# A streaming-encoder trunk on one core: the order of the transfers in the feed-forward is fixed by hand

## The chip, the core and the metric

The kernel runs on one core of a Trainium2 chip. A core has five engines that work side by side, each through its own queue of instructions: TensorE (PE: matrix products, with its weight loads shown as PEld), VectorE (DVE), ScalarE (ACT), GpSimd (POOL) and SyncE (SP), which here does nothing but issue transfers from the chip's memory into the core's buffer. An engine begins an instruction when the one before it has gone and the semaphores that it waits for have been reached. The metric is the time of one execution on the device, in microseconds (us).

## The reference

```
DEPTH, D_MODEL, D_FF, SEQ = 2, 1024, 2816, 512
for i in range(DEPTH):
    h = rmsnorm(x, mix_norm[i])
    x = x + (pool_mixer(h, ...) if i % 2 == 0 else chunk_attention(h, ...))
    h = rmsnorm(x, ffn_norm[i])
    x = x + conv_ffn(h, ffn_w_gate[i], ffn_w_val[i], ffn_conv_w[i], ffn_conv_b[i], ffn_w_out[i])

def conv_ffn(h, w_gate, w_val, conv_w, conv_b, w_out):
    a = h @ w_gate                                    # (512, 1024) @ (1024, 2816)
    ap = pad(a, two frames in front)
    a = ap[:, 0:S] * conv_w[0] + ap[:, 1:S+1] * conv_w[1] + ap[:, 2:S+2] * conv_w[2] + conv_b
    return (silu(a) * (h @ w_val)) @ w_out            # (512, 2816) @ (2816, 1024)
```

One batch of 512 frames goes through two layers: a pooling mixer, a feed-forward, a chunked attention, a second feed-forward. Everything is in 32-bit floats. The change concerns the two feed-forwards only.

## The kernel before, in words

The activations lie channel by channel: X[0] to X[7] hold 128 channels by 512 frames each. To keep 32-bit accuracy, every operand of a product is split into a high part and a low part (ACT copies the high part, line 409, and DVE subtracts it for the low part, line 410), and a product is the sum of up to three matmuls: high by high, high by low, low by high (lines 123 to 125).

A feed-forward (`ffn`) has 22 tiles of 128 hidden channels. Of each tile f come two outputs, the gate and the value, from two weight blocks `gv[l, f, 0]` and `gv[l, f, 1]` of 512 KB. From the sixth tile on both outputs are computed together by a scheme of seven half-size products (`strassen`). It works in named steps: `load` issues the two transfers into the buffers `gv_r`, `s1` to `s4` build sums of the weight blocks on DVE, `h1` to `h4` copy the high parts on ACT, `l1` to `l4` make the low parts on DVE, `b11`, `b21`, `t1`, `t2`, `t3`, `t4`, `b22` are the products on PE (lines 610 and 612), and `a1`, `v1`, `x1` are ACT's copies of the bank `st_m` (line 619, into `a`, `v` and `w`) between the products that add into that bank: `t1` may start only when `v1` has read it. `a3` (line 763) copies the last half and `a4` (line 768) adds to it on DVE. `c0` to `c6` are the convolution, the silu and the split of the result (lines 421 to 435).

The second product of the feed-forward (`output`) runs in four groups of hidden tiles, `OUT = ((0, 5), (5, 6), (11, 6), (17, 5))`, each with eight blocks of 128 output channels. A block needs a weight transfer of 320 or 384 KB (`wo_r`), its high part on ACT (`ow_h`, line 409) and its low part on DVE (`ow_l`, line 410), then 15 or 18 matmuls (`out`), and an addition to X on DVE (line 817). These blocks are strewn among the products of the later tiles: `tour` yields at the points of a tile, and behind each point the loop takes as many matmuls of the waiting group as `due` says. A block's transfer and its high part are issued in the program when the block before it begins; its low part comes two tiles of matmuls later.

The order of work is set in three ways. What stands in a block `tc.manual_schedule(engines=...)` keeps the order of the program on the engines named. For the rest a planner chooses: it lays out the program against its own model of time and issues on each queue what is ready there. Buffers come from pools with a set number of copies: three for `gv_r` (tag `wr`), one for `wo_r` in the first three groups (tag `or`), two for `ow_h` and two for `ow_l`; a transfer into a buffer waits until the last reader of what was there has finished. For `gv_r` of tile f + 1 that is `s4` of tile f (line 675) and `l4` of tile f - 1 (line 721); for the next `wo_r` it is the low part of the block before (line 410).

PE is in fixed order through the whole feed-forward. The order within a tile is written by hand in `PLACES`, seven places to a tile, where q, o, f and n stand for the tile two before, the one before, this one and the next:

```
PLACES = ("o.x1 q.c5 f.s2 o.x2 f.s3 o.x3 f.b11", "f.a1 f.h2 f.s4 o.l4 q.c6 n.load o.b22", "o.a3 f.h3 f.l2 o.a4 f.b21", "o.c0 f.a2 f.l3 f.a5 o.t4",
          "n.h1 f.h4 o.c1 o.v3 o.c2 o.v4 f.t2", "f.v1 o.c3 n.l1 f.v2 f.t3", "n.s1 o.c4 f.t1")
```

From the first place of tile 8 (`ORDERED`) to the fourth place after the last tile, DVE and ACT also keep this order. SP does not: there the planner chooses.

Of the kernel before, what the change touches and what calls it, by code (L numbers as in the profile page):

```python
# [72 lines left out]
def trunk(ctx: ExitStack, tc: tile.TileContext, xt, xT, cols, band, edge, poolw, gv, wout, wqk, wv, wo, rel, out):  # L73
# [291 lines left out]
    ET = mybir.EngineType  # L365
# [15 lines left out]
    def ffn(l, first, pool, acc, summed=None):  # L381
# [140 lines left out]
        def plain(f):  # L522

            o = []
            for i in range(2):
                with ExitStack() as after:
                    if f < 4:
                        for x in (made, seed) if l == 0 else (known if f == 2 and i == 0 else made,):
                            after.enter_context(tc.issue_after(x.ins))
                    hi, lo = ready[f][i] if f in ready else weights(f, i)  # L530
                o.append(psum("S", f"gv{l}_{f}_{i}", 4))
                for k in range(KD):
                    s = slice(k * P, (k + 1) * P)
                    mm = run(mm3(o[i], hi[:, s], lo[:, s], *(slots[c][4 * (k % 4) + k // 4] for c in range(2)), k == 0, k == KD - 1))
                    if k % 2 and k < KD - 1:
                        yield mm
                if i == 0:
                    yield mm
            run(hidden(f, o[0], lambda c: nc.vector.tensor_mul(c, o[1], c)))
            yield mm  # L540
# [280 lines left out]
        def tour():  # L821

            tiles = {}

            def steps_of(f):
                if f not in tiles:
                    tiles[f] = strassen(f) if f < NF and KIND[f - 1] == "s" else {}
                return tiles[f]

            def place(f, k):  # L830

                for word in PLACES[k].split():
                    x, name = word.split(".")
                    step = steps_of(f + "qofn".index(x) - 2).get(name)
                    if step:
                        step()

            for f in range(KIND.index("s"), NF + 2):
                if f == KIND.index("s"):
                    for g in range(f):  # L840
                        if KIND[g] == "p":
                            yield from plain(g)
                    for j, _ in enumerate(apart(f)):
                        for k, name in ((2, "load"), (4, "h1"), (5, "l1"), (6, "s1")):
                            if j == k:
                                steps_of(f + 1)[name]()
                        yield
                    continue
                for k in range(7):
                    if (f, k) == (ORDERED, 0):  # L850
                        order.enter_context(tc.manual_schedule(engines={ET.DVE, ET.Activation}))
                    place(f, k)
                    if steps_of(f - 1 if k in (1, 3) else f):
                        yield
                    if (f, k) == (NF, 3):
                        order.close()

        with tc.manual_schedule(engines={mybir.EngineType.PE}):
            h, seed, known, made = early()
            queue, left, n = [], 0, 0  # L860
            order = ExitStack()
# [7 lines left out]
            seq += [(NF - 1, False), (NF - 1, True)]  # L869
            ends = [seq.index((b + m - 1, True)) + 1 for b, m in OUT]  # L870
            steps = tour()
            for g, (b, m) in enumerate(OUT):
                points = ends[g] - (ends[g - 1] if g else 0)
# [354 lines left out]
```

## Time and profile before

| | |
|---|---|
| time, median of 3 runs | 991.06 us (989.55 to 991.6) |
| the profiled execution | 991.02 us, of which the span from the first to the last instruction is 989.2 us |
| first feed-forward, ordered stretch | about 127 to 331 us of the span |
| second feed-forward, ordered stretch | about 726 to 931 us of the span |
| PE, DVE, ACT busy | 968.9, 805.4, 573.8 us |
| granted TensorE clock, mean | 0.993 |

A row of the timeline gives the start in us from the span's beginning, the duration in us, the engine (SPq is SP's queue, where the duration is that of the issue alone), the line of the kernel, the operation, what is written and read, the shapes, how many instructions the row joins, and in brackets the idle time of the engine before the row with what ended it. A row of the waits reads: who waited for whom, us in total, how often, the longest. A row of the windows gives a stretch, its length, the busy time of PE, PEld, DVE, ACT and POOL with their counts, the granted clock as a share of full speed, the share of the DMA engines that was busy, and GB/s.

### The profile page before, as it was taken

To read this page: it belongs to the slowest core of one execution; us is meant where nothing else is said; L and a number is where in the kernel's file an instruction comes from. 1 tells how busy PE (TensorE), PEld (TensorE's weight loads), DVE (VectorE), ACT (ScalarE), POOL (GpSimd) and SP (SyncE) were. 2 spreads that over 40 slices of the span, in tenths; PEclk is the share of its full clock that TensorE was granted. 3 is DMA by queue.
4 is the path that set the end of the run, shared out by engine and by line. 5 is a ranking of instruction groups with operands and counts; after the bars stand their busy time and mean duration, and the time that the engine had idled before them with its cause. 6 is when DMAs were issued, how large, how long until landed. Compare 5 with 4: busy or idle time off the path is not lost.

```text
span 989.2 us, 13813 instructions
## 1 busy us (share of the span) xinstructions
PE 968.9 (98%) x5038; PEld 822.3 (83%) x5038; DVE 805.4 (81%) x1452; ACT 573.8 (58%) x990; POOL 103.2 (10%) x90
## 2 busy tenths in 40 slices
PE   8999999899989999999999999999999899989998
PEld 7788988788878888888888787888988788878886
DVE  8999989799879854442777887899979899879953
ACT  7665565565546444345898987656545465446531
POOL 2300000000000013204535441000000000000000
PEclk9999999999999999999999999999999999989999
DMA  8222332332323224232343242332423223222323
GB/s 336 80 86 81 100 112 86 104 115 93 102 75 117 72 83 148 89 123 87 117 125 96 84 116 75 99 107 78 126 70 115 101 83 125 75 101 75 104 84 112
DMA packets 37428, 102.83 MB, mean 104 GB/s; under 512 B 4432, under 2 KB 7904, under 8 KB 37360
## 3 DMA queue, kind: packets, MB, share of 16 engines
q1 hardware_dynamic: 37296, 101.90, 31.5%
q8 instruction: 40, 0.66, 0.3%
q14 instruction: 28, 0.23, 0.1%
q0 software_dynamic: 32, 0.04, 0.0%
q10 hardware_dynamic: 32, 0.00, 0.0%
HBM read 95.60 MB, written 2.14 MB: 99 GB/s over the span
## 4 chain that ended last, share of the span: by engine, by line
PE 91%; DVE 5%; ACT 2%; issue 1%; DMA 0%; DVEq 0%; ACTq 0%
PE st_m L610 9%; PE out L125 8%; PE out L123 8%; PE out L124 8%; PE st_t L610 5%; PE st_m L612 5%; PE gv L124 4%; PE gv L123 4%; PE gv L125 4%; PE qk L124 3%; PE qk L123 3%; PE qk L125 3%; PE st_b L610 3%; PE st_t L612 2%; PE tp L1059 2%; PE oo L1071 2%
## 5 line engine op out<-in xcount | busy, mean ns | idle before, releaser
L409 ACT ACTIVATE ow_h<-wo_r 128x640 fp32r<-128x640 f32 (+1 forms) x64 | 50.5, 788 | 81.3 <-PE out L124 47.2
L125 PE MATMUL out<-one,ow_l 128*128 128x512 f32 x224 | 88.2, 394 | 5.6 <-DVE ow_l L410 5.6
L123 PE MATMUL out<-one,ow_h 128*128 128x512 f32 x224 | 88.1, 393 | 0.0
L124 PE MATMUL out<-one,ow_h 128*128 128x512 f32 x224 | 88.0, 393 | 0.0
L817 DVE TENSOR_TENSOR X<-out,X 128x512 f32<-128x512 f32 (+1 forms) x65 | 44.2, 681 | 49.8 <-PE out L125 49.3
L610 PE MATMUL st_m<-two,g_h 128*128 128x512 f32 x224 | 70.0, 394 | 0.0
L610 PE MATMUL st_m<-h,g_h 128*128 128x512 f32 x224 | 69.1, 389 | 0.0
L410 DVE TENSOR_TENSOR ow_l<-wo_r,ow_h 128x640 fp32r<-128x640 f32 (+1 forms) x64 | 56.6, 885 | 2.6 <-ACT ow_h L409 2.6
L424 DVE SCALAR_TENSOR_TENSOR c<-a,col,c 128x511 f32<-128x511 f32 (+1 forms) x76 | 56.4, 745 | 0.0
L125 PEld LDWEIGHTS out<-one,ow_l 128*128 128x128 f32 x224 | 42.4, 189 | 12.7 <-DVE ow_l L410 6.5
L125 PE MATMUL qk<-wqk_h,two 128*128 128x512 f32 x128 | 51.4, 402 | 0.0
L123 PE MATMUL qk<-wqk_h,two 128*128 128x512 f32 x128 | 50.8, 409 | 0.0
L124 PE MATMUL qk<-wqk_l,two 128*128 128x512 f32 x128 | 50.8, 397 | 0.0
L610 PEld LDWEIGHTS st_m<-h,g_h 128*128 128x128 f32 x224 | 42.1, 188 | 9.6
L612 PEld LDWEIGHTS st_m<-two,g_l 128*128 128x128 f32 x224 | 42.0, 188 | 8.9
L610 PEld LDWEIGHTS st_m<-two,g_h 128*128 128x128 f32 x224 | 41.1, 188 | 9.3 <-ACT w L619 0.8
L619 ACT ACTIVATE w<-st_m 128x512 f32<-128x512 f32 x28 | 16.7, 597 | 54.2 <-PE st_m L612 54.2
L124 PEld LDWEIGHTS out<-one,ow_h 128*128 128x128 f32 x224 | 42.5, 190 | 6.3 <-DVE one L435 0.3
L123 PEld LDWEIGHTS out<-one,ow_h 128*128 128x128 f32 x224 | 42.5, 190 | 6.0
L1047 DVE CUSTOM_DVE_ANT_0 sb<-sc,B 128x128 f32<-128x128 f32 (+1 forms) x64 | 31.1, 486 | 18.8 <-PE sc L1044 18.1
L612 PE MATMUL st_m<-h,g_l 128*128 128x256 f32 x224 | 45.1, 283 | 0.0
L148 POOL TENSOR_TENSOR n_acc<-n_acc,n_sq 128x512 f32<-128x512 f32 x7 | 9.6, 1366 | 336.1 <-ACT n_sq L146 336.1
(378 smaller groups left out, 3027.2 us busy)
## 6 DMA issues: line engine op xcount, KB each, us to landing
gv_r<-gv SPq DMA_DIRECT2D x86, 512.0 KB, 3.8
wo_r<-wout SPq DMA_DIRECT2D x32, 384.0 KB, 3.1
wo_r<-wout SPq DMA_DIRECT2D x32, 320.0 KB, 2.9
wqk_r<-wqk SPq DMA_DIRECT2D x16, 512.0 KB, 3.5
wv_r<-wv SPq DMA_DIRECT2D x8, 512.0 KB, 3.4
wo_r<-wo SPq DMA_DIRECT2D x8, 512.0 KB, 3.4
xt<-xt SPq DMA_DIRECT2D x4, 512.0 KB, 5.7
X<-xT SPq DMA_DIRECT2D x8, 256.0 KB, 7.6
```

The lines of the kernel that those rows point to most:

```text
L123: yield nc.tensor.matmul(o, sh, mh, start=first, stop=False, **how)
L124: yield nc.tensor.matmul(o, sh, ml, start=False, stop=False, **how)
L125: yield nc.tensor.matmul(o, sl, mh, start=False, stop=last, **how)
L409: nc.scalar.activation(hi[:, :n], raw[:, :n], AF.Copy)
L410: return hi, lo, lambda: nc.vector.tensor_sub(lo[:, :n], raw[:, :n], hi[:, :n].bitcast(F32))
L424: nc.vector.scalar_tensor_tensor(c[:, j:], a[:, :S - j], cw[2 - j], c[:, j:], op0=OP.mult, op1=OP.add)
L610: nc.tensor.matmul(o, hi[:, c], B[i, name], start=first and i == 0, stop=False, **how)
L612: nc.tensor.matmul(o[:, 0], lo[:, c], B[i, name][:, 0], start=False, stop=i == 3, **how)
L817: nc.vector.tensor_add(X[d][:, fs], o[:, fs], X[d][:, fs])
L1047: nc.vector.tensor_tensor_reduce(out=s_[:, :n], in0=sc[:, :n], in1=BT[h % 2][:, :n][:, ::-1], scale=1.0, scalar=3e38, op0=OP.add, op1=OP.m ...
L1059: nc.tensor.transpose(tp[:, j * P:(j + 1) * P], s_[:, j * P:(j + 1) * P], ident)
L1071: nc.tensor.matmul(oo[:, j * P:], V[j, h // 4][:, h % 4].rearrange("p a d -> p (a d)"), PT[e][c][:, 4 * j:3 * j + TT].rearrange("p t q -> ...
```

## The change

SP joins DVE and ACT in the block that fixes the order, so the transfers that are issued there, the pairs `gv_r` and the blocks `wo_r`, keep the order in which the program names them. The stretch is the same as before, in both feed-forwards.

```
                 for k in range(7):
                     if (f, k) == (ORDERED, 0):
-                        order.enter_context(tc.manual_schedule(engines={ET.DVE, ET.Activation}))
+                        order.enter_context(tc.manual_schedule(engines={ET.DVE, ET.Activation, ET.SP}))
                     place(f, k)
```

More of the change, by code (lines that the diff above doesn't have):

```diff
@@ L850, in tour @@
                     if (f, k) == (ORDERED, 0):
-                        order.enter_context(tc.manual_schedule(engines={ET.DVE, ET.Activation}))
+                        order.enter_context(tc.manual_schedule(engines={ET.DVE, ET.Activation, ET.SP}))
                     place(f, k)
```

## The prediction

> **What bounds the kernel now.** I read the first part of the page (busy time by engine), then the waits of PE between 127 and 331 us, the stretch that the change covers in the first of the two feed-forward layers.
>
> ```profile
> PE 968.9 (98%) x5038; PEld 822.3 (83%) x5038; DVE 805.4 (81%) x1452; ACT 573.8 (58%) x990; POOL 103.2 (10%) x90
> PE out L125 <- DVE ow_l L410: 5.6, 2, 2.8
> 203.00:266.00 63.00, 63.00 (x328) 53.81 (x327) 58.77 (x95) 34.72 (x50) 0.00 (x0) 1.00 0.31 105
> ```
>
> The first row: PE works 98% of the span. The second row, of the waits: in that stretch PE stands still twice, 2.8 us each, and both times for DVE's low part of the first weight block of an output group; nothing else stops it. The third, of the windows (PE, PEld, DVE, ACT, POOL busy): over four tiles PE is busy all 63 us and DVE 58.77, so DVE has 63.00 - 58.77 = 4.23 us to spare, 1.06 a tile; ACT is idle nearly half the time. No transfer bounds anything here. So the change can gain little, and what it can lose is the head start of the transfers.
>
> **The order on the transfers' row now.** The timeline of SP, the same stretch (a row joins several issues; the number behind x counts them):
>
> ```profile
> 160.99 0.33 SPq L391 DMA_DIRECT2D wo_r<-wout  x1
> 171.06 15.12 SPq L391 DMA_DIRECT2D gv_r<-gv  x4
> 187.28 17.08 SPq L391 DMA_DIRECT2D wo_r<-wout  x3
> 204.60 0.93 SPq L391 DMA_DIRECT2D gv_r<-gv  x2
> 214.30 0.33 SPq L391 DMA_DIRECT2D wo_r<-wout  x1
> 218.24 0.93 SPq L391 DMA_DIRECT2D gv_r<-gv  x2
> 244.18 0.33 SPq L391 DMA_DIRECT2D wo_r<-wout  x1
> 248.97 0.93 SPq L391 DMA_DIRECT2D gv_r<-gv  x2
> 256.34 0.33 SPq L391 DMA_DIRECT2D wo_r<-wout  x1
> 265.81 15.34 SPq L391 DMA_DIRECT2D gv_r<-gv  x4
> ...
> 760.47 0.33 SPq L391 DMA_DIRECT2D wo_r<-wout  x1
> 770.53 15.12 SPq L391 DMA_DIRECT2D gv_r<-gv  x4
> ```
>
> I counted the program's order out of `PLACES`, `seq`, `ends`, `WAIT` and the `due` line. From tile 8 on it is, with one "gv" for a pair and g.d for block d of output group g: gv9, 0.5, gv10, 0.6, 0.7, gv11, gv12, 1.0, gv13, 1.1, 1.2, gv14, 1.3, gv15, 1.4, 1.5, gv16, 1.6, gv17, 1.7, gv18, 2.0, gv19, 2.1, 2.2, gv20, 2.3, gv21, 2.4, 2.5. The rows show another order: 1.0 goes at 160.99, ahead of gv12 at 171.06; 1.3 is the last of the three from 187.28 and goes just before gv14 at 204.60; 1.4 at 214.30 before gv15; 1.7 at 244.18 before gv17; 2.0 at 256.34 before gv18. In all eight of a layer's output blocks (0.6, 1.0, 1.3, 1.4, 1.6, 1.7, 2.0, 2.4) now overtake a pair that the program names first; no pair overtakes a block. The second layer has the same order (its last two rows are 1.0 and gv12, gv13).
>
> **The change part by part.** No transfer and no instruction is added or removed, and PE, DVE and ACT were in fixed order before. Eight issues a layer move, all of them later, behind a pair whose second half waits for tile buffers that DVE frees. Behind a moved issue on SP stands only the next block or pair, which waits for later work of DVE anyway. The pairs gain a little by going first; nothing waits for them, so I price that at nothing (their cover is the tile of time before L651 reads them).
>
> When does a moved block land? Alone, the page says, a block takes about 3 us. Behind a pair it takes longer; two cases in this trace show it, the first blocks after gv13 and gv19 (SP's issue of the pair, then ACT's start, ended by the landing):
>
> ```profile
> wo_r<-wout SPq DMA_DIRECT2D x32, 384.0 KB, 3.1
> 185.25 0.93 SPq L391 DMA_DIRECT2D gv_r<-gv  x2
> 191.20 0.85 ACT L409 ACTIVATE ow_h<-wo_r 128x768 fp32r<-128x768 f32 x1 [5.87 <-DMA wo_r<-wout]
> 280.22 0.93 SPq L391 DMA_DIRECT2D gv_r<-gv  x2
> 287.28 0.85 ACT L409 ACTIVATE ow_h<-wo_r 128x768 fp32r<-128x768 f32 x1 [6.97 <-DMA wo_r<-wout]
> ```
>
> From the pair's first issue to the landing: 191.20 - 185.25 = 5.95 and 287.28 - 280.22 = 7.06 us, with the block issued 2.0 us after the pair's first. A moved block goes as soon as the pair has gone, about 1.2 us after its first issue, so it queues behind the same bytes. Bounds: not before 1.2 + 3.1 = 4.3, not after 7.06. I take 6.2, near the shorter of the two rows, which have the same 1.4 MB in flight. The Trainium skill ("DMA: Bandwidth & Descriptors", section "Anatomy of one DMA") fits a transfer to a fixed 2.0 us plus bytes at 436 GB/s, measured on GpSimd's path; for 1.44 MB in one row that is an estimate of 5.3 us, earlier than both rows here, and by it the sum below would be about nothing.
>
> ACT is in fixed order, so the copy `ow_h` that reads the block holds up all of ACT behind it, up to the copy `v` (L619) that empties the bank `st_m`. PE's next product into that bank (step `t1`) may not begin before. ACT's rows at five of the places, and PE's `t1` after each:
>
> ```profile
> 174.42 0.83 ACT L409 ACTIVATE ow_h<-wo_r 128x768 fp32r<-128x768 f32 x1
> 178.53 0.60 ACT L619 ACTIVATE v<-st_m 128x512 f32<-128x512 f32 x1 [1.81 <-PE st_m L612]
> 179.68 0.63 PE L610 MATMUL st_m<-two,g_h 128*128 128x512 f32 x2
> 208.00 0.84 ACT L409 ACTIVATE ow_h<-wo_r 128x768 fp32r<-128x768 f32 x1
> 210.21 0.58 ACT L619 ACTIVATE v<-st_m 128x512 f32<-128x512 f32 x1
> 212.74 0.62 PE L610 MATMUL st_m<-two,g_h 128*128 128x512 f32 x2
> 218.24 0.83 ACT L409 ACTIVATE ow_h<-wo_r 128x768 fp32r<-128x768 f32 x1
> 221.48 0.82 ACT L421 ACTIVATE c<-a,col 128x512 f32<-128x512 f32 x1 [1.19 <-DVE a L768]
> 225.75 0.60 ACT L619 ACTIVATE v<-st_m 128x512 f32<-128x512 f32 x1 [1.99 <-PE st_m L612]
> 228.74 0.62 PE L610 MATMUL st_m<-two,g_h 128*128 128x512 f32 x2
> 250.95 0.85 ACT L409 ACTIVATE ow_h<-wo_r 128x768 fp32r<-128x768 f32 x1 [1.00 <-PE out L124]
> 257.51 0.60 ACT L619 ACTIVATE v<-st_m 128x512 f32<-128x512 f32 x1 [1.86 <-PE st_m L612]
> 260.50 0.62 PE L610 MATMUL st_m<-two,g_h 128*128 128x512 f32 x2
> 269.17 0.83 ACT L409 ACTIVATE ow_h<-wo_r 128x768 fp32r<-128x768 f32 x1
> 273.51 0.60 ACT L619 ACTIVATE v<-st_m 128x512 f32<-128x512 f32 x1 [2.00 <-PE st_m L612]
> 274.65 0.63 PE L610 MATMUL st_m<-two,g_h 128*128 128x512 f32 x2
> ```
>
> Late by = pair's issue + 6.2 - start of `ow_h`. Slack = ACT's idle time up to `v` (in brackets) + the time from the end of `v` to `t1`.
>
> - 1.0: 171.06 + 6.2 - 174.42 = 2.84; slack 1.81 + 0.55 = 2.36; PE waits 0.48.
> - 1.3: 204.60 + 6.2 - 208.00 = 2.80; slack 0 + 1.95; PE waits 0.85.
> - 1.4: 218.24 + 6.2 - 218.24 = 6.20; slack 1.19 + 1.99 + 2.39 = 5.57; PE waits 0.63.
> - 1.7: 248.97 + 6.2 - 250.95 = 4.22; slack 1.86 + 2.39 = 4.25; nothing.
> - 2.0: 265.81 + 6.2 - 269.17 = 2.84; slack 2.00 + 0.54 = 2.54; PE waits 0.30.
>
> The other three (0.6, 1.6, 2.4) come to 0 to 0.1 by the same count, which I leave out.
>
> What carries over. At 1.4 and 1.7 `ow_h` stands ahead of the copy `a` (L763), for which DVE waits; the like place at 191 shows what that does to DVE:
>
> ```profile
> 192.35 0.42 DVE L768 TENSOR_TENSOR a<-a,st_m 128x256 f32<-128x256 f32 x1 [3.96 <-ACT a L763]
> ```
>
> So at 1.4 I estimate that DVE loses 4.0. PE shifts by 0.63 itself, and two tiles give 2.1 back (1.06 each): some 1.2 is left when 1.7 comes, with no slack over, and PE waits 1.2. At 1.7 DVE loses about half as much, 2, and with what is left 1.7 more is late at 2.0: 0.30 + 1.7 = 2.0. Some 6 us after that comes one of PE's two old waits for DVE, and a PE that arrives later waits less there: I give 1.0 of the 2.0 back. The same swallows the 0.48 at 1.0. Per layer 0.85 + 0.63 + 1.2 + 1.0 = 3.7 us. Bounds of the carry: none (1.5 = 0.85 + 0.63 alone), or all of it kept, some 6 more.
>
> The clock. The windows around three of the old waits of 2.8 us (the seventh number is the granted clock):
>
> ```profile
> 185.00:190.00 5.00, 2.69 (x14) 2.30 (x15) 3.39 (x5) 0.34 (x1) 0.00 (x0) 1.00 0.73 254
> 280.00:285.00 5.00, 2.72 (x7) 2.24 (x8) 3.36 (x5) 0.30 (x1) 0.00 (x0) 0.68 0.73 257
> 885.00:890.00 5.00, 5.00 (x18) 4.13 (x18) 1.05 (x3) 2.20 (x4) 0.00 (x0) 0.56 0.24 86
> ```
>
> The same wait costs nothing at 187, (1 - 0.68) x 2.72 = 0.9 us at 282, and (1 - 0.56) x 5.00 = 2.2 us after 882. New waits of 0.6 to 2 us are shorter, so from 0 to 2.2 each; I take 0.25 for four of them, 1.0 a layer. The Trainium skill ("TensorE: Matmul & The Clock Gate", "Part 1: The HAM clock gate") says that the clock is halved after an idle window of about 3.4 us that runs freely; read strictly, no new wait is long enough and this 1.0 would be 0, yet the rows show drops behind waits of 2.8.
>
> **Sum.** 3.7 + 1.0 = 4.7 us a layer, 9.4 us for both. The profiled execution took 991.02 us (span 989.2), the median of the runs is 991.06: the same. 991.0 + 9.4 = 1000.4 us.
>
> **The rivals.**
>
> 1. The late transfers stay hidden: no change, 991.0. It decides at the landing. PE first waits where `ow_h` plus slack is passed: 174.42 + 2.36 - 171.06 = 5.72 us behind the pair's issue at 1.0, and in the same way 5.35 at 1.3, 5.57 at 1.4, 6.23 at 1.7, 5.90 at 2.0. So a block that lands within 5.35 us of the pair's first issue costs nothing anywhere, and this lies between my bounds of 4.3 and 7.06. For it: the 5.95 row, whose block went 0.8 us later than a moved one would; and ACT's waits of 5.87 and 6.97 stopped PE nowhere. Against it: those two places lie just behind a PE wait of 2.8, where ACT has that much more time. The Trainium skill's fit above, 5.3 us, falls just on this side.
> 2. Faster, by the clock. The two old waits a layer get shorter because PE has lost some time just before, and the clock that drops behind them stays up: 0.9 and 2.2 us in the rows above, 3 to 4 with the other layer's, so 987 us. It needs a landing under about 5.5, where waits at `t1` remain below half a us; above it those waits cost more than the clock returns. That the old waits themselves go is out: `ow_l` of a first block is late by DVE's own row, which is full ahead of it, not by its transfer, which was issued at 160.99 and read at 174.42.
> 3. Much slower: the block lands at 7.06 and DVE's lag is not worked off. Each late-by grows by 0.86: 1.34, 1.71, 1.49, 0.83 and 1.16 by the slacks, 5.2 without the first, and about 5 of carry: 10 a layer, 1011 us.
> 4. The order does not change, because the planner's order counts as the program's: 991.0. Against it: the eight overtakings, which a row fixed in program order cannot hold.
>
> **How the numbers follow.** My forecast 0.60; rival 1 0.14; rival 2 0.06; rival 3 0.18; rival 4 0.02. Slower by over 0.2% (2 us, about what the spread of the runs, 989.55 to 991.6, can tell): 0.78; within it 0.16; faster 0.06. The forecast alone covers 995 to 1006; the range reaches from rival 1 to rival 3: 990.5 to 1012.
>
> **What would show it.** In the trace after: on SP every block of the eight stands behind its pair; ACT's idle time before `ow_h` that ends with the transfer goes from 2 places to some 6 to 8 in a layer's stretch and from 5.87 + 6.97 = 12.8 us in total to about 30; PE has new waits at L610 of `st_m` for ACT's `v`, in tiles 11, 13, 14, 16 and 17, and its waits for `ow_l` shrink from 2.8 to about 2. Each layer is longer by nearly the same. The prediction is wrong if the blocks land at 5.3 or sooner, if ACT or DVE works the lag off faster than 1 us a tile, or if the attention between the layers is planned otherwise and moves by itself.

## The result and the profile after

The changed kernel takes 1004.02 us (median of 4 runs, 1001.37 to 1004.86); the kernel before, beside it, 991.33 us. The ratio is 1.0126, with a 95% interval of 1.0102 to 1.0149: slower by 12.7 us. The profiled execution took 1003.79 us, with a span of 1001.9 us, 12.7 more than the 989.2 before, so the trace holds all of the loss.

The page after: the busy times, then two groups (busy, mean ns of one | idle time ahead of them, its releaser), then the transfers of the large blocks (KB each, median us from issue to landing).

```profile
PE 972.8 (97%) x5038; PEld 821.5 (82%) x5038; DVE 804.4 (80%) x1452; ACT 572.5 (57%) x990; POOL 103.2 (10%) x90
L409 ACT ACTIVATE ow_h<-wo_r 128x640 fp32r<-128x640 f32 (+1 forms) x64 | 50.6, 790 | 124.7 <-DMA wo_r<-wout 83.1
L610 PE MATMUL st_m<-two,g_h 128*128 128x512 f32 x224 | 72.4, 405 | 14.6 <-ACT v L619 14.5
wo_r<-wout SPq DMA_DIRECT2D x32, 384.0 KB, 4.5
```

No engine has more work; the same 5038 matmuls stand in a longer span. The third row is new: ahead of the products into `st_m` PE now idles 14.5 us for ACT's copy `v`. The second says what ACT waited for: 83.1 us for transfers of output blocks, ahead of `ow_h`, where it was 28.6 before. The last row was 3.1 before and is 4.5.

The waits of PE, then those of ACT ahead of `ow_h` and of DVE for ACT's `a`, from 127 to 340 us (first layer):

```profile
PE st_m L610 <- ACT v L619: 5.1, 6, 2.0
PE out L125 <- DVE ow_l L410: 3.6, 2, 1.9
ACT ow_h L409 <- DMA wo_r<-wout: 39.0, 11, 6.8
DVE a L768 <- ACT a L763: 18.2, 4, 4.9
```

and from 726 to 950 us (second layer):

```profile
PE st_m L610 <- ACT v L619: 9.4, 6, 3.1
PE out L125 <- DVE ow_l L410: 2.8, 2, 1.7
```

The old waits of PE on `ow_l`, 5.6 us in each layer, shrank to 3.6 and 2.8; the new ones for `v` are 5.1 and 9.4. Net that is +3.1 and +6.6, 9.7 of the 12.7 us. By the first row PE is also 972.8 - 968.9 = 3.9 us longer busy, with the same instructions; the two come to 13.6, and elsewhere PE idles 0.9 less. Compared matmul by matmul, there are 15 places where `t1` is now held up, three of them with next to no wait; at each the matmul ahead counts as busy about 0.16 us longer and the first one behind about 0.10, 4 us in all. So such a stop costs about 0.26 us more than the wait that is counted for it.

On SP all eight blocks stand behind their pairs, in both layers. Three places, each the pair's first issue and then ACT's `ow_h`; the first two are 1.3 and 1.4 of the first layer, the last is 1.3 of the second with PE's `t1` behind it:

```profile
204.59 0.93 SPq L391 DMA_DIRECT2D gv_r<-gv  x2
211.79 0.85 ACT L409 ACTIVATE ow_h<-wo_r 128x768 fp32r<-128x768 f32 x1 [3.74 <-DMA wo_r<-wout]
220.06 0.93 SPq L391 DMA_DIRECT2D gv_r<-gv  x2
226.18 0.85 ACT L409 ACTIVATE ow_h<-wo_r 128x768 fp32r<-128x768 f32 x1 [6.00 <-DMA wo_r<-wout]
811.69 0.93 SPq L391 DMA_DIRECT2D gv_r<-gv  x2
819.58 0.84 ACT L409 ACTIVATE ow_h<-wo_r 128x768 fp32r<-128x768 f32 x1 [4.43 <-DMA wo_r<-wout]
821.79 0.57 ACT L619 ACTIVATE v<-st_m 128x512 f32<-128x512 f32 x1
822.42 1.01 PE L610 MATMUL st_m<-two,g_h 128*128 128x512 f32 x2 [3.12 <-ACT v L619]
```

The last four rows are the whole mechanism: `ow_h` starts 7.9 us after the pair's first issue, ACT has stood idle for the block, the copy `v` comes after it on ACT, and PE has waited 3.12 us for `v`. From the pair's first issue to the start of `ow_h` it took 7.2, 6.1 and 7.9 us at the three places.

### The profile page after: what moved, and what is told of

The parts are those of the page before. It is cut to its first block, busy times and chain, and to the rows that moved or that the text cites. A ratio compares the mean times of both kernels' runs of the same rounds, so it can differ in the third digit from the quotient of the medians.

```text
span 1001.9 us, 13807 instructions
## 1 busy us (share of the span) xinstructions
PE 972.8 (97%) x5038; PEld 821.5 (82%) x5038; DVE 804.4 (80%) x1452; ACT 572.5 (57%) x990; POOL 103.2 (10%) x90
## 4 chain that ended last, share of the span: by engine, by line
PE 64%; DVE 21%; DMA 7%; ACT 4%; issue 3%; SPq 0%; DVEq 0%; ACTq 0%
DMA wo_r<-wout 7%; PE out L124 5%; PE out L125 5%; PE out L123 5%; PE st_m L610 4%; PE gv L124 3%; PE gv L125 3%; PE gv L123 3%; PE qk L124 3%; PE qk L123 3%; PE qk L125 3%; DVE g_l L410 3%; PE st_m L612 2%; DVE ow_l L410 2%; PE st_t L610 2%
## 5 line engine op out<-in xcount | busy, mean ns | idle before, releaser
L409 ACT ACTIVATE ow_h<-wo_r 128x640 fp32r<-128x640 f32 (+1 forms) x64 | 50.6, 790 | 124.7 <-DMA wo_r<-wout 83.1
L610 PE MATMUL st_m<-two,g_h 128*128 128x512 f32 x224 | 72.4, 405 | 14.6 <-ACT v L619 14.5
L1047 DVE CUSTOM_DVE_ANT_0 sb<-sc,B 128x128 f32<-128x128 f32 (+1 forms) x64 | 31.1, 485 | 18.9 <-PE sc L1044 18.1
L421 ACT ACTIVATE c<-a,col 128x512 f32<-128x512 f32 x38 | 30.6, 810 | 26.0 <-DVE a L768 24.6
L612 PE MATMUL st_m<-two,g_l 128*128 128x256 f32 x224 | 44.8, 282 | 0.0
```

The costliest lines, as they stand in the source:

```text
L409: nc.scalar.activation(hi[:, :n], raw[:, :n], AF.Copy)
L421: nc.scalar.activation(c, a, AF.Identity, scale=cw[2], bias=cw[3])
L610: nc.tensor.matmul(o, hi[:, c], B[i, name], start=first and i == 0, stop=False, **how)
L612: nc.tensor.matmul(o[:, 0], lo[:, c], B[i, name][:, 0], start=False, stop=i == 3, **how)
L1047: nc.vector.tensor_tensor_reduce(out=s_[:, :n], in0=sc[:, :n], in1=BT[h % 2][:, :n][:, ::-1], scale=1.0, scalar=3e38, op0=OP.add, op1=OP.m ...
```

## The experiments

My theory was the one of the prediction: the place of the eight blocks behind their pairs is the cause, ACT's fixed row brings the lateness to `v`, and part of it is handed on from one tile to the next. Against it stood three rivals: that holding SP's row costs by itself, that a late block costs at DVE and PE whoever copies it, and that each place costs on its own.

### 1. The row fixed, the old order

```
+EARLY = ((0, 6), (1, 0), (1, 3), (1, 4), (1, 6), (1, 7), (2, 0), (2, 4))
...
                     if i == 2 and d + 1 < KD:
                         w[d + 1][2]()
+                        then = (g, d + 2) if d + 2 < KD else (g + 1, 0)
+                        if then in EARLY:
+                            issue(*then)
```

`issue` is the transfer alone, taken out of `load`. SP's order is then the order of the kernel before, held by hand.

> The transfers' row stays fixed, but the program issues each of the eight moved blocks (0.6, 1.0, 1.3, 1.4, 1.6, 1.7, 2.0, 2.4) right behind the low part of the block before it, so that SP's order is the one of the kernel before while everything else is the changed kernel. Theory 1 (the eight blocks' place behind their pairs is the whole cause): 991 us within 2, PE's waits on L610 for ACT's v are gone, and ACT's waits ahead of ow_h for a transfer are back at about 2 places and 13 us a stretch. Rival (holding the row costs by itself, whatever its order): 997 us or more, with new idle time on SP or ACT while the order is the old one.

Measured: 991.31 us, ratio to the kernel before 0.9999 (0.9985 to 1.0012). Waits in the first layer, of PE and of ACT:

```profile
PE out L125 <- DVE ow_l L410: 5.6, 2, 2.8
ACT ow_h L409 <- DMA wo_r<-wout: 14.9, 3, 6.8
```

PE has only its old wait again, and ACT's waits for blocks are down from 39.0 to 14.9. Holding the row costs nothing; the order does.

### 2. Late transfers, but ACT's copy later in its row

```
                     if i == 2 and d + 1 < KD:
+                        if g < len(OUT) - 1:
+                            high(d + 1)
                         w[d + 1][2]()
```

`high` is the copy `ow_h`, which `load` no longer makes, except for the last group and for each group's first block.

> Transfers in the changed kernel's order; only ACT's high copy of a block (ow_h) goes later in its fixed row, from the block's load to just ahead of its low part, in groups 0 to 2 except for the first block of each group. So ACT reaches v in the place of the moved blocks without waiting for the transfer. Theory 1 (the lateness reaches PE through ACT's row: high copy, then v, then the add on VectorE, then st_m at t1): PE's waits for v stay only at the first blocks (tiles 11 and 17), 1 to 3 us a layer, ACT's waits ahead of ow_h for a transfer are under 8 us a stretch, 993 to 996 us. Rival (the block itself is late for its low part and its products, whoever copies it): waits of PE on ow_l or ow_h take the place of those on v, 1001 to 1005 us.

Measured: 988.53 us, ratio 0.9981 (0.9968 to 0.9994). Waits of PE in the first layer, then of ACT:

```profile
PE out L125 <- DVE ow_l L410: 5.1, 2, 2.8
PE st_m L610 <- ACT v L619: 0.3, 1, 0.3
ACT ow_h L409 <- DMA wo_r<-wout: 14.7, 7, 4.6
```

All the transfers are as late as in the changed kernel, and PE hardly waits for `v`. The rival would have put new waits on `ow_h` or `ow_l` in their place; there are none, only the two old ones on `ow_l`, a little shorter. So the transfers did not cost by being late for the products, but by the place of the copy in ACT's row. I had expected 993 to 996 us; that was too high, since the first blocks (1.0 and 2.0), whose copies kept their place, cost 0.3 us in the first layer and 0.9 in the second, not 1 to 3. ACT still waits 14.7 us for blocks, where I had expected under 8, and DVE waits 8.2 us for `ow_h`; PE hardly feels it, since the copy `v` no longer stands behind.

### 3 and 4. Half of the blocks early

`EARLY` is cut to the first four or to the last four of the eight.

> Blocks 0.6, 1.0, 1.3, 1.4 are issued early again as in the kernel before; 1.6, 1.7, 2.0, 2.4 stay behind their pairs. In the changed kernel PE lost 1.1 to 1.5 us in tile 16 and 2.2 to 2.9 in tile 17, less 1.0 to 1.7 from the shorter wait on ow_l. Carry theory (of the prediction: most of what tiles 16 and 17 lose is lateness handed on from the blocks before by ACT and VectorE): with the first four early, tile 16 loses under 0.5 and tile 17 under 1.0, 991 to 993 us. Rival (each late block costs where it lies): tiles 16 and 17 keep 1.1 to 1.5 and 2.2 to 2.9 us, 995 to 998 us.

> Blocks 1.6, 1.7, 2.0, 2.4 are issued early as in the kernel before; 0.6, 1.0, 1.3, 1.4 stay behind their pairs. Both theories: tiles 11, 13, 14 keep their new waits of 0.8 to 1.5, 0.7 to 3.3 and 0.2 us, the old wait on ow_l in tile 11 stays about 1 us shorter. Carry theory: the halves don't add up; this one costs 5 to 9 us (996 to 1000 us) and together with the other half it stays 3 us or more under the 12.7 of the whole. Rival (local): 4 to 7 us (995 to 998 us), and the two halves together come to the whole, 12 to 13.

Measured: with the last four late 992.81 us, ratio 1.0025 (1.0007 to 1.0043); with the first four late 994.26 us, ratio 1.0035 (1.0021 to 1.0048). The waits of PE for `v`, first with the last four late (first layer, second layer):

```profile
PE st_m L610 <- ACT v L619: 2.4, 2, 1.5
PE st_m L610 <- ACT v L619: 2.5, 2, 2.4
```

then with the first four late:

```profile
PE st_m L610 <- ACT v L619: 0.7, 1, 0.7
PE st_m L610 <- ACT v L619: 4.8, 4, 1.6
```

By the ratios the halves cost 2.5 and 3.5 us, 6.0 together, against 12.5 of the whole (1.26% of 991): about half of the loss is there only when both halves are late. The intervals of the three leave this open by some 3 us, not in its sign. That is the carry, and its place shows: in the kernel with all eight late PE waited in tile 16, behind the block 1.7, 0.9 and 1.3 us; with the first four early there is no wait in tile 16 at all. The landing alone does not explain this. PE is ready for a `t1` at its start less its wait; with the first four early that is 11.5 us after the pair's first issue in tile 16, as in the kernel before, and `ow_h` starts 5.9 and 6.2 us after it. With all eight late `ow_h` starts only a little later, 6.4 and 6.5 us after the pair's first issue, but PE is ready after 10.2 and 10.0. As `t1` can start 4.8 us after `ow_h` there, even 6.5 would have been in time for 11.5. So that wait was lateness from the tiles before, by which the pair itself went out later against PE.

In tile 17 I was wrong: I expected under 1.0 and PE waited 1.5 and 2.4. That part comes from the last four themselves. The total of the run with the first four late fell below both my ranges.

### 5. The landing alone: between the two transfers of a pair

```
-                raws = [raw_tile(f"gv{l}_{f}_{i}", gv[l, f, i]) for i in range(2)]
+                raws = [raw_tile(f"gv{l}_{f}_0", gv[l, f, 0])]
+                if f in BETWEEN:
+                    issue(*BETWEEN[f])
+                raws.append(raw_tile(f"gv{l}_{f}_1", gv[l, f, 1]))
```

`BETWEEN` maps the eight tiles to their blocks.

> The eight blocks go between the two transfers of their pairs instead of behind both (first half of the pair, block, second half), the rest as in the changed kernel. This moves the landing alone, to about 5 us after the pair's first issue by the spacing of issues (0.6 us one transfer earlier) against the 6.1 measured in the changed kernel. Theory (the loss starts from a landing of about 5.35 us on, as the prediction's rival 1 put it): 991 to 994 us, PE's waits on L610 for ACT's v under 2 us a layer. Rival (any transfer ahead of the block on the row already costs most of it): 997 to 1001 us, waits of 4 us or more a layer.

Measured: 990.99 us, ratio 1.0004 (0.9988 to 1.002). A block still waits behind 512 KB, yet the loss is gone. Of the 16 moved blocks 15 land 4.4 to 5.5 us after the pair's first issue, one at 6.0. This is block 2.0 in the second layer (SP's issue of the pair's first half, ACT, then PE's `t1`), the same place in the kernel before (SP's issue and `t1`), and the waits of PE in that layer of the experiment:

```profile
869.93 0.33 SPq L391 DMA_DIRECT2D gv_r<-gv  x1
875.91 0.85 ACT L409 ACTIVATE ow_h<-wo_r 128x768 fp32r<-128x768 f32 x1 [2.52 <-DMA wo_r<-wout]
878.76 0.73 PE L610 MATMUL st_m<-two,g_h 128*128 128x512 f32 x2 [1.30 <-ACT v L619]
```

```profile
866.75 0.93 SPq L391 DMA_DIRECT2D gv_r<-gv  x2
875.59 0.63 PE L610 MATMUL st_m<-two,g_h 128*128 128x512 f32 x2
```

```profile
PE st_m L610 <- ACT v L619: 1.6, 2, 1.3
```

875.91 - 869.93 = 5.98 us: the only block of the 16 clearly past the limits that rival 1 of the prediction set (5.90 for 2.0), and PE waits 1.3 us right behind it. But 0.08 us past the limit do not make a wait of 1.3. PE is ready for `t1` 878.76 - 1.30 - 869.93 = 7.53 us after the pair's first issue, where it was 875.59 - 866.75 = 8.84 in the kernel before. The pair went out 1.3 us late against PE, and in this layer DVE, which frees the pair's buffers, waits 15.2 us for ACT's `a`, against 8.7 in the kernel before.

The layer's other wait is 0.3; the first layer, where all land by 4.7, has none. So the 1.5 us by which the pair's second half puts off the landing decide whether this change costs anything: landings up to 5.5 us after the pair's first issue held up PE nowhere. A fixed threshold this is not, since the slack shrinks where the pair is late against PE.

### 6. Early transfers and the late copy

Edits 1 and 2 together.

> Transfers in the old order (each of the eight blocks early) and ACT's high copy late in its row, as in the run before last of this kind. If the order of the transfers costs only through ACT's row, this equals the kernel with late transfers and the late high copy, 988.5 us: 987 to 990 us. If the late transfers still cost something by themselves there, this one is faster, 984 to 987 us.

Measured: 990.53 us, ratio 0.9995 (0.9981 to 1.0009), half a microsecond above the range of 987 to 990. No faster than with the late transfers (988.53), so once the copy stands late the order of the transfers costs nothing here, with PE's old waits still in place. The 2 us between the two are about what these runs can tell, and the profiled spans (986.5 and 986.2 us) show no difference.

### 7. The old waits: the first block's low part two places earlier

From here on the experiments aim at PE's four old waits of 2.8 us, which all the kernels above have in some form.

```
             w[0][2]()
+            yield
             for d in range(KD):
...
                     wait = WAIT[g]
+                    if g and at == (0, 3, 3, 3)[g]:
+                        next(queue[0])
```

> Old order of the transfers, and VectorE makes the low part of the first block of groups 1 and 2 two places earlier in its fixed row, for PE's waits of 2.8 us on ow_l in tiles 11 and 17 of both layers, which the kernel before has too. Theory A (those waits and the drops of the granted clock behind them are removed): the four waits are 11.2 us, the drops behind them some 1.3 to 2.9 us in three of four places, 975 to 981 us. Theory B (only the waits go, the clock drops elsewhere): 979 to 982 us. Rival (VectorE is late for another step in the same place, which PE waits for instead): 985 us or more.

Measured: 995.29 us, ratio 1.0047 (1.0027 to 1.0066): slower, as the rival had it, though not for the rival's reason. The waits of PE in the first layer, then what stands ahead of the second of them (SP's issues, ACT):

```profile
PE st_m L610 <- ACT v L619: 7.0, 2, 3.6
```

```profile
284.18 0.93 SPq L391 DMA_DIRECT2D gv_r<-gv  x2
289.95 0.85 ACT L409 ACTIVATE ow_h<-wo_r 128x768 fp32r<-128x768 f32 x1 [5.67 <-DMA wo_r<-wout]
294.08 0.58 ACT L619 ACTIVATE v<-st_m 128x512 f32<-128x512 f32 x1
```

The four waits on `ow_l` are gone and come back 10 to 14 us later as four waits of 3.0 to 4.3 us for `v`. It is the mechanism of this change again: the second block of the group, 2.1, lies behind the pair of tile 19 in every order, the old one too, and holds up ACT. Before, PE stood still for 2.8 us just then, and that was its cover.

### 8. The same with late transfers and the late copy

> Transfers in the changed kernel's order, ACT's high copies late, and the low part of the first block of groups 1 and 2 two places earlier on VectorE. Theory: the gains add, 988.5 less the 11 us of the four old waits, 975 to 980 us. Rival (the first block lands too late in this order for its low part two places earlier, so VectorE waits for it and hands that on): 982 to 990 us, with waits of VectorE ahead of ow_l.

Measured: 982.82 us, ratio 0.9927 (0.9903 to 0.995). About as the rival had it. PE's old waits are gone; its waits for `v` are 4.0 and 3.2 us a layer (longest 2.1), and DVE waits 11.2 and 12.0 us for ACT's `ow_h` ahead of `ow_l`: the late landings are handed on. The waits of PE and of DVE in the first layer:

```profile
PE st_m L610 <- ACT v L619: 4.0, 3, 2.1
DVE ow_l L410 <- ACT ow_h L409: 11.2, 6, 4.5
```

### 9 and 10. The second block early as well

Experiment 7, and behind the low part of the first block the second one is issued, ahead of its pair; then the same with the late copy.

```
             w[0][2]()
+            if g in (1, 2):
+                issue(g, 1)
             yield
```

> The kernel with the old order and the low parts of the first blocks two places earlier (995.3 us; the four old waits gone, but PE waits 3.0 to 4.3 us for ACT's v some 10 us later), and now also the second block of groups 1 and 2 (1.1 and 2.1) is issued right behind that low part, ahead of its pair. Theory (there, too, a block behind its pair holds ACT's high copy and v behind it): the waits for v go, and ACT's waits of about 6 us ahead of ow_h with them, 975 to 982 us. Rival (VectorE's row, made fuller in that place by the low part, is what makes v's successor late): the waits for v stay at 2 us or more, 988 to 996 us.

> All together: the eight blocks and 1.1 and 2.1 early, the low part of the first blocks two places earlier, ACT's high copies late in its row. Theory: no wait of PE for v or ow_l of 0.5 us or more is left in the two stretches, 974 to 980 us. Rival (with the waits gone the granted clock falls more, or VectorE's row takes over as the bound): 981 to 985 us, as the kernel with late transfers in the same arrangement (982.8).

Measured: 972.80 us, ratio 0.9822 (0.9807 to 0.9837), and 972.72 us, ratio 0.9819 (0.9802 to 0.9835). Both beat the kernel before by 1.8%, below the ranges that I had given. Of experiment 9, ACT's two waits for blocks that are left in the first layer, then the windows over the ordered stretches (PE, PEld, DVE, ACT, POOL busy, granted clock), then the whole run's span and clock:

```profile
ACT ow_h L409 <- DMA wo_r<-wout: 0.5, 2, 0.3
```

```profile
127.00:320.00 193.00, 193.00 (x1026) 165.83 (x1025) 182.56 (x292) 111.42 (x161) 0.00 (x0) 1.00 0.32 105
712.00:905.00 193.00, 193.00 (x1034) 166.19 (x1033) 179.10 (x288) 110.96 (x162) 0.00 (x0) 1.00 0.31 103
```

```profile
core 0: 971.1 us, clock 1.000
```

PE is busy all 193 us of each stretch. With no block behind its pair at the places that matter, the late copy has nothing left to give, so 9 and 10 are equal.

## Why the prediction was right

The forecast was 1000.4 us in a range of 990.5 to 1012; measured were 1004.02. Sign and mechanism held. The first layer's waits came out near the number (net 3.1 us against 3.7), in part by luck, as the single places show; the second layer's are 6.6 against 3.7, and that is the miss: the layers did not lengthen alike. The 2.0 us put down to the clock were not there, while the stops cost some 4 us beside the counted waits, which the sum did not have. In the first layer ACT waited for blocks 11 times, 39.0 us in all, where I had 6 to 8 times and about 30.

- **The order.** Each of the eight blocks went behind its pair, as counted out from the program; PE, ACT and DVE run the same instructions in the same order as before.
- **The landing, taken as 6.2 us.** In the first layer the eight start `ow_h` 5.8 to 7.2 us after the pair's first issue, 6.2 on average; in the second 5.9 to 7.9, on average 6.65. So 6.2 was the right middle, but one value for all of them was not: 1.3 lands latest in both layers and its tile 13 in the second layer lost 3.12 us where 0.85 stood in the sum. Experiment 5 shows that the landing decides whether the change costs anything. Rival 1's thresholds (5.35 to 6.23) held only roughly, as they were read from one layer with DVE on time: with the last four early, in the first layer, `ow_h` of 1.3 and 1.4 started 5.93 and 6.22 us after the pair's first issue, past 5.35 and 5.57, and PE did not wait; in experiment 5 it waited 1.3 at 0.08 past. The Trainium skill ("DMA: Bandwidth & Descriptors", "Anatomy of one DMA") would have it at 5.3 us by its fit; the rows say 5.8 and up, so the trace does not agree. By the figure that the same page gives for reads from the chip's memory ("Where 436 GB/s comes from", about 358 GB/s in place of 436) the estimate is 6.0, near the first layer's 6.2. The profile's page of the kernel before has 2.9, 3.1 and 3.5 us for transfers of 320, 384 and 512 KB (`wo_r` and `wqk_r`); the same estimate gives 2.9, 3.1 and 3.5 with 358 GB/s, and 2.8, 2.9 and 3.2 with 436.
- **The waits at `t1`.** The forecast had them in tiles 11, 13, 14, 16 and 17: 0.48, 0.85, 0.63, 1.2 and 2.0 us. The first layer's trace has 0.67, 0.59, none of its own in 14, 0.90 and 2.04, and 0.17 and 0.76 in tiles 15 and 18, which I had at nothing: 5.1 in all against 5.2. The second has 1.38, 3.12, none, 1.33 and 2.70, with 0.51 in tile 9 and 0.37 in tile 20: 9.4. That tiles 11 and 13 of the first layer came near is luck. At 1.0 `ow_h` started 5.84 us after the pair's first issue, not 6.2, which alone leaves 0.1 of the 0.67; the rest is lag handed on from 0.6. At 1.3 it started 1.0 us later than 6.2, but PE was ready for `t1` 9.46 us after the pair's first issue and not 212.74 - 204.60 = 8.14, as the sum had it.
- **The step that was mis-sized** is the count of tile 13 in the second layer, twice over. Its `ow_h` started 1.7 us later than 6.2, and I let the carry begin only at 1.4. The rows of the two kernels there (`ow_h` of the changed kernel, at 819.58, is shown above):

```profile
806.88 0.82 ACT L421 ACTIVATE c<-a,col 128x512 f32<-128x512 f32 x1 [1.61 <-DVE a L768]
808.79 0.85 ACT L409 ACTIVATE ow_h<-wo_r 128x768 fp32r<-128x768 f32 x1 [1.09 <-PE out L124]
811.38 0.62 PE L610 MATMUL st_t<-two,g_h 128*128 128x512 f32 x2
```

```profile
814.33 0.81 ACT L421 ACTIVATE c<-a,col 128x512 f32<-128x512 f32 x1 [1.61 <-DVE a L768]
816.82 0.62 PE L610 MATMUL st_t<-two,g_h 128*128 128x512 f32 x2
```

  The first fence is the timeline of the kernel before, the second that of the changed one. ACT's `c` is 814.33 - 806.88 = 7.45 us later than before, while PE's products next to it are 816.82 - 811.38 = 5.44 later. So ACT was already 2.0 us behind PE when the block 1.3 was due, and its idle time ahead of `ow_h` grew by 4.43 - 1.09 = 3.3 more. Less the 2.1 us between `v` and `t1` before, that is 3.2, and PE waited 3.12.

  That lag begins at 0.6, one of the three blocks that I had left out as coming to 0 to 0.1. Behind the next moved block, 1.0, PE was ready for `t1` 179.68 - 171.06 = 8.62 us after the pair's first issue before the change; with 0.6 late it was 8.0 in the first layer and 7.5 in the second, both in the changed kernel and with only the last four early. With 0.6 early again (the first four early) it was back at 8.62 in both layers. The sum counted the blocks from their pairs' issues in the old trace, and so put the pairs' own lateness at nothing up to 1.4.
- **The carry** is shown by experiments 3 and 4: tile 16's wait is carry alone, as forecast (1.2, measured 0.9 and 1.3), and about half of the loss needs both halves. That it starts from ACT's row is shown by experiment 2, where PE is ready for `t1` at 2.0 as long after the pair's first issue as before, 8.84 and 9.01 us. How it goes on, the rows at 2.0 in the changed kernel show (DVE, SP's pair, ACT, PE's `t1`; first layer):

```profile
271.43 0.68 DVE L675 TENSOR_TENSOR sb<-gv_r,sa 128x512 f32<-128x512 f32 x1
272.18 0.93 SPq L391 DMA_DIRECT2D gv_r<-gv  x2
278.01 0.85 ACT L409 ACTIVATE ow_h<-wo_r 128x768 fp32r<-128x768 f32 x1 [2.37 <-DMA wo_r<-wout]
280.85 0.73 PE L610 MATMUL st_m<-two,g_h 128*128 128x512 f32 x2 [2.04 <-ACT v L619]
```

  The pair goes when DVE's `sb` is done, and DVE is late from its waits for ACT's `a`, which doubled (9.0 to 18.2 us in the first layer). PE is ready 280.85 - 2.04 - 272.18 = 6.63 us after the pair's first issue, against 274.65 - 265.81 = 8.84 before: 2.2 of lag where the sum had 1.7. So 5.83 us from the pair to `ow_h`, within rival 1's 5.90, still cost 2.04. With the last four late alone PE is ready after 7.28 and 7.04 us, so most of the lag at 2.0 comes from 1.6 and 1.7; which of the two, no run separates.
- **What the old waits give back**, 1.0 a layer and the 0.48 of tile 11, 1.5 together: 5.6 - 3.6 = 2.0 and 5.6 - 2.8 = 2.8. Too little by 0.5 us in the first layer and 1.3 in the second, which hid part of the miss on the new waits.
- **The clock**, 1.0 a layer: not confirmed. The mean granted clock is 0.994 after and 0.993 before. The extra drops behind new waits and the missing ones behind shorter old waits came out about even. The 3.0 us of the 12.7 that are not waits are not the clock's, then: they lie mainly at the stops, some 4 us in the matmuls ahead of and behind them, as told with the result. That the forecast had 2.0 for the clock in that place is luck.
- **Rival 2**, faster by the clock, was ruled out for this order by the landings, but its idea that the clock stays up where the waits are gone is what experiments 8 to 10 show, below.
- **"That the old waits themselves go is out"** held for this change. It also led me to take them as given; experiments 7 to 10 show that they were worth more than everything that the order of the transfers could cost.

## What to carry to other kernels

A transfer's place in a queue is worth what stands behind its first reader on that reader's engine: before fixing a row, measure for each transfer the landing from the issue of what now goes first, and compare it with the reader's slack; here 1.5 us decided between no loss and 1.3%. Take that slack as an upper bound: it shrank by up to 2.2 us where the pair itself went out late. If the transfer cannot go earlier, move its first reader behind the urgent work of its engine: that alone gave back all of the loss. And when a wait is taken away, look at once for what was late under its cover, as the second blocks were here: without them that step cost 0.5%, with them it gained 1.8%.

## What the runs showed of the hardware

Behind some waits of PE the granted clock drops, so that they cost more than their length. Windows of 5 us (the third number from the end is the granted clock) in the changed kernel, behind a wait of 1.87 us, around the end of one of 2.04, and behind 3.12; then in experiment 7 behind one of 3.4:

```profile
187.00:192.00 5.00, 5.00 (x17) 4.15 (x18) 1.00 (x1) 0.84 (x2) 0.00 (x0) 0.66 0.62 238
280.00:285.00 5.00, 4.15 (x23) 3.62 (x24) 5.00 (x9) 3.48 (x7) 0.00 (x0) 1.00 0.00 0
822.00:827.00 5.00, 4.58 (x15) 3.84 (x16) 4.82 (x8) 2.00 (x4) 0.00 (x0) 0.66 0.00 0
```

```profile
200.00:205.00 5.00, 5.00 (x20) 4.03 (x19) 5.00 (x9) 2.47 (x4) 0.00 (x0) 0.71 0.00 0
```

A wait of 1.87 us was followed by a drop and one of 2.04 was not; the two drops shown of the changed kernel cost (1 - 0.66) x 5.00 = 1.7 us each. They come and go between executions at the same place: the prediction's window 185 to 190 shows none behind a wait of 2.8, while experiment 1, with the same order and wait, has 0.66 from 188 to 193. The runs of the kernel before, beside the experiments, have mean clocks from 0.990 to 0.998. In the profiled executions the mean is 0.993 in the kernel before with four waits of 2.8 us, 0.990 in experiment 7 with four of 3.0 to 4.3, 0.999 in experiment 8 with none over 2.1, and 1.000 where no wait is left. The span of experiment 9 is 989.2 - 971.1 = 18.1 us shorter than that of before; the four waits are 11.2 of it, and 0.007 of 989.2, 6.9 us, is the clock. A price for each microsecond waited does not follow: in the changed kernel PE waits 20.9 us for `v` and `ow_l`, nearly twice the 11.2, most of it in shorter pieces, and its clock is 0.994. The Trainium skill ("TensorE: Matmul & The Clock Gate", "Part 1: The HAM clock gate") speaks of an idle window of about 3.4 us; here drops follow waits of half that length.

The other surprise is the spread of one transfer: the same 384 KB behind the same two of 512 KB landed between 5.8 and 7.8 us after the first issue, block 1.3 latest in both layers of the changed kernel (7.1 and 7.8). With the last four early, where 1.3 stands behind its pair just the same, it landed at 5.85 and 6.30, and there 1.4 of the second layer was latest, at 7.4. What makes a block 1 to 2 us slower in some places stays open.
